# A hybrid attention and state-space block on one core: the attention branch's gate in blocks of 1024 columns, four of its sixteen k-tiles with seven tile products for eight

## Chip, core and metric

The kernel runs on one core of a Trainium2 chip. The metric is the device time of one execution in microseconds (us). Before the change the median of three runs is 1970.81 us (1970.03 to 1972.08).

Engines are named as in the profile: PE is TensorE (PEld its weight loads), DVE VectorE, ACT ScalarE, POOL GpSimd, SP SyncE.

## What is computed

One residual layer for a sequence of 256 tokens and a width of 2048, in float32: two token mixers side by side (sparse attention with a small indexer, and a Mamba-2 state-space mixer), each multiplied by a sigmoid gate, then a SwiGLU channel mixer and a last RMSNorm. The part that matters here:

```python
    gates = jax.nn.sigmoid(u @ w_gate).reshape(bsz, seq, 2, D_MODEL)
    merged = gates[:, :, 0] * (y_attn @ w_attn_branch) + gates[:, :, 1] * (y_ssm @ w_ssm_branch)
    return merged @ w_out
```

`u` is the normalized input (256 x 2048) and `w_gate` is 2048 x 4096. Its first 2048 columns are the gate of the attention branch.

## The kernel before

**A product in three matmuls.** Every float32 operand of the large gemms is split into a high part, rounded to the type that PE takes in one pass (an ACT copy), and a low part, the rest (a DVE subtraction). A tile product is then three matmuls that add into one psum buffer: high x high, high x low, low x high (L165 to L167). The 256 tokens are two token tiles t of 128; the contraction of 2048 is sixteen k-tiles of 128.

**A plain gemm** (`gemm`) computes 512 output columns: two psum buffers (one for each t), four loads of 1 MB on the SP queue (four k-tiles each, tile raw, three buffers), for each load two pairs of hi and lo tiles of 1024 columns (L196, L197), and 16 x 2 x 3 = 96 matmuls. The hi and lo tiles have four buffers each; behind the mixers every fifth pair lies in the pool xtra instead.

**Seven products.** The feed-forward gemms use `block7` with `fetch`: 1024 columns at once, as two blocks of 512. Four k-tiles are a quad. In a quad marked 1 two of its k-tiles, two token tiles and two column blocks form a 2 x 2 by 2 x 2 block product that Winograd's form of Strassen's scheme computes with seven tile products (numbered 1 to 7, each with a psum buffer) in place of eight. It needs sums of the left-hand tiles (slots 1, 8, 9, 12) and of the weights: `fetch` makes them on DVE as ta and tb (L749 to L751) and splits raw, tb and ta (L730, L731). The other two k-tiles of the quad, and quads marked 0, take eight products. When all is summed, DVE adds the psum buffers together into the four output blocks. The down projection (`down7`) has an eighth psum buffer, p8, for part of the eight-product terms.

**Order of work.** The instructions of each engine stand in a fixed order, which the framework's planner lays down when the program is built: it takes instructions as their operands and buffers come free by its own estimates, by priority, and priority is program order. Loads and splits of weights are raised by `high_priority`. PE, ACT, DVE and the SP and POOL queues each work through their order one by one.

**Around the change.** The attention loop runs over j = 0 to 3 (four heads each). For each j: a gemm for q (`w_m`), the transposes of q, and for t = 0, 1: logits lg (L618), masking into sc (L621), maximum (L626), exponentials (L629), division (L632, L633), transposes of sc (L641), their split into pT (L214, L215), and av (L645 to L647), which reads the value tile vh. av is split into ya_hi and ya_lo. Then comes a gemm of the state-space gate (`w_g`, blocks 4 to 7), evicted with a sigmoid at L655. Behind the loop the four blocks of the attention gate follow as plain gemms into the four tiles sga (a sigmoid at L667, `w_g` blocks 0 to 3), then the branch projection (`w_ab`, from ya_hi and ya_lo), the merge, the transposes of the merged tiles (`trans_split`), the output projection (`w_o`) with `quad_ops` for the left-hand operands of the feed-forward, and the feed-forward.

**Buffers.** The pool big has 11 tiles of 8 KB in a partition; u_hi, u_lo (two tiles each), acc (two), ya_hi, ya_lo (two each) and vh (one) are among them. The pool mid has 8 tiles of 4 KB. Psum: mm (4), trp (2, transposes and the like) and sdp (2, logits and av) up to the end of `w_o`; then they are closed and mmf (7) and trf (1) take their place, with waits tile by tile:

```python
    pctx.close()
    mm = ctx.enter_context(tc.tile_pool(name="mmf", bufs=7, space=bass.MemoryType.PSUM, reuse_waits="tile"))
    trp = ctx.enter_context(tc.tile_pool(name="trf", bufs=1, space=bass.MemoryType.PSUM, reuse_waits="tile"))
```

Of the kernel before, what the change touches and what calls it, by code (L numbers as in the profile page):

```python
# [8 lines left out]
F32 = mybir.dt.float32  # L9
# [5 lines left out]
P = 128  # L15
# [24 lines left out]
QUADS = (1, 1, 1, 0)  # L40

# [23 lines left out]
def hybrid_block(ctx, tc, xt, x, consts, cols, heads, gfin, w_a, w_i, w_m, w_g, w_ab, w_sb, w_o, w_f1, w_f2, out):  # L65
# [658 lines left out]
    def halves(raw, cuts):  # L724

        out = {}
        for i, n in cuts:
            hi, lo = (v[:, : n * 512] for v in hl_tiles())
            src = raw[:, i : i + n, :].rearrange("p k n -> p (k n)")
            nc.scalar.activation(hi, src, AF.Copy)  # L730
            nc.vector.tensor_tensor(lo, src, hi.bitcast(F32), ALU.subtract)  # L731
            for j in range(n):
                out[i + j] = hi[:, j * 512 : (j + 1) * 512], lo[:, j * 512 : (j + 1) * 512]
        return out

    nts = [0]

    def fetch(w, i, seven):

        with tc.high_priority(PRE):  # L740
            raw = wraw.tile([P, 4, 512], F32, tag="raw", name=nm("raw"))
            nc.sync.dma_start(raw.rearrange("p k n -> p (k n)"), w[i])
            if not seven:
                return halves(raw, ((0, 2), (2, 2)))
            b = halves(raw, ((0, 2),))
            nts[0] += 1
            ta = mid_t([P, 2, 512], name="ta")
            tb = mid_t([P, 2, 512], name="tb") if nts[0] % 2 else xtra[0].tile([P, 2, 512], F32, tag="tb", name=nm("tb"))
            nc.vector.tensor_tensor(ta, raw[:, 2:4, :], raw[:, 1:3, :], ALU.subtract)  # L749
            nc.vector.tensor_tensor(tb[:, 0, :], raw[:, 3, :], ta[:, 0, :], ALU.subtract)  # L750
            b["last"] = nc.vector.tensor_tensor(tb[:, 1, :], raw[:, 0, :], tb[:, 0, :], ALU.subtract)  # L751
            for base, t in ((6, tb), (4, ta)):
                for j, v in halves(t, ((0, 2),)).items():
                    b[base + j] = v
            b.update(halves(raw, ((3, 1),)))
            return b

# [29 lines left out]
    def block7(w, first, quads, get, ahead=None, after=None):  # L787

        n7 = sum(quads)
        n1 = 4 * len(quads) - 2 * n7
        left = {i: 3 * n7 for i in (1, 6, 7)}
        left.update({i: 3 * (n7 + n1) for i in (2, 3, 4, 5)})
        if after is not None:
            left[5], left[8] = 3 * n7, 3 * n1
        ps = {}

        def prod(i, a, b):
            start = i not in ps
            if start:
                ps[i] = tr_t([P, 512], "p8") if i == 8 else mm.tile([P, 512], F32, tag="mm", name=nm(f"p{i}"))
            with tc.issue_after(after) if i == 8 and start else nullcontext():
                for j, (x, y) in enumerate(((a[0], b[0]), (a[0], b[1]), (a[1], b[0]))):
                    left[i] -= 1
                    nc.tensor.matmul(ps[i], x, y, start=start and j == 0, stop=left[i] == 0)  # L808

        order = [(q, part) for q in range(len(quads)) for part in range(2)]  # L810
        if after is not None:
            order[1:3] = order[2:0:-1]
        for q, part in order:
            seven = quads[q] and part == 0
            if q == part == 0 and ahead is not None:
                b = ahead
            else:
                b = fetch(w, first + 2 * q + part, seven)
            if seven:
                prod(1, get(q, 0), b[1])  # L820
                prod(2, get(q, 2), b[0])
                prod(6, get(q, 9), b[6])
                prod(4, get(q, 3), b[7])
                prod(7, get(q, 1), b[5])
                prod(5, get(q, 8), b[4])
                prod(3, get(q, 12), b[3])
                continue
            k0 = 4 if quads[q] else 4 * part
            d0 = 10 if quads[q] else 8 + 2 * part
            a1, a2, d = (lambda k: k0 + 2 * k), (lambda k: k0 + 2 * k + 1), (lambda k: d0 + k)  # L830
            for i, slot, n in ((2, a1, 0), (4, a2, 0), *(((8, a2, 1), (3, a1, 1)) if after is not None else ((5, a2, 1), (3, d, 1)))):
                for k in range(2):
                    prod(i, get(q, slot(k)), b[2 * k + n])
        return ps
# [232 lines left out]
```

## Time and profile before

| | |
|---|---|
| median of three runs | 1970.81 us |
| the profiled execution | 1969.88 us, of which the span from the first to the last instruction is 1967.9 us |
| mean granted clock of PE | 0.998 |
| PE busy | 1954.5 us (99% of the span), 9095 matmuls |
| DVE, ACT busy | 1499.9 us (76%), 1066.8 us (54%) |
| read from HBM | 372 MB, 190 GB/s over the span |

How to read it: busy time of PE is from a matmul's start to its modelled end, and matmuls overlap, so one of 512 columns is listed with some 390 ns though they follow each other more closely. An engine's idle time is put down to what released it. `out<-in` are names of tiles, `mm<-hi,uh` a matmul into a buffer mm from the weights' tile hi and the left-hand tile uh.

### The profile page before, as it was taken

How to read it: one execution, taken by the hardware profiler on the slowest of the kernel's cores; microseconds unless marked ns; L12 is line 12 of the kernel's file. 1: busy time of each engine (PE TensorE's matmuls, PEld its weight loads, DVE VectorE, ACT ScalarE, POOL GpSimd, SP SyncE). 2: the span in 40 equal slices, each digit the busy share in tenths (PEclk: the TensorE clock that was granted, in tenths of full speed). 3: DMA queues.
4: the chain of work that ended last, by engine and by line, in shares of the span. 5: the costliest groups of instructions: out<-in, count | busy, mean ns of one | idle time of the engine just before them, and what ended most of it. 6: DMA issues, size and time to landing. Idle time of an engine off the chain costs nothing. (4 is left out here: it accounts for less than half of the span.)

```text
span 1967.9 us, 23619 instructions
## 1 busy us (share of the span) xinstructions
PE 1954.5 (99%) x9095; PEld 1619.2 (82%) x9095; DVE 1499.9 (76%) x2050; ACT 1066.8 (54%) x1291; POOL 36.2 (2%) x87
## 2 busy tenths in 40 slices
PE   9999999999999999999999999999999999999998
PEld 7898888888888888888888888788888888888886
DVE  7898867778778766666654556788989999899964
ACT  6575564654654544555554445565555665555553
POOL 0000000000000000000000000000000000000000
PEclk9999999999999999999999999999999999999999
DMA  7645555555554545544555555455545555555553
GB/s 276 233 151 177 189 195 187 190 195 171 193 203 160 193 171 192 182 163 168 185 185 195 184 193 206 154 198 212 193 178 208 213 194 213 192 195 213 212 193 128
DMA packets 54432, 375.71 MB, mean 191 GB/s; under 512 B 6304, under 2 KB 6816, under 8 KB 10672
## 3 DMA queue, kind: packets, MB, share of 16 engines
q1 hardware_dynamic: 51120, 360.86, 51.8%
q0 software_dynamic: 1968, 11.60, 1.7%
q10 hardware_dynamic: 1232, 1.75, 0.2%
q8 instruction: 71, 1.16, 0.2%
q14 instruction: 41, 0.34, 0.1%
HBM read 372.02 MB, written 2.16 MB: 190 GB/s over the span
## 5 line engine op out<-in xcount | busy, mean ns | idle before, releaser
L197 DVE TENSOR_TENSOR lo<-raw,hi 128x1024 fp32r<-128x1024 f32 (+3 forms) x449 | 540.5, 1207 | 314.6 <-ACT hi L196 313.1
L196 ACT ACTIVATE hi<-raw 128x1024 fp32r<-128x1024 f32 (+3 forms) x449 | 468.8, 1047 | 529.9 <-PE mm L167 463.4
L166 PE MATMUL mm<-lo,uh 128*128 128x512 f32 (+2 forms) x1184 | 461.0, 389 | 0.0
L167 PE MATMUL mm<-hi,ul 128*128 128x512 f32 (+2 forms) x1184 | 458.2, 388 | 0.2 <-DVE ul L218 0.2
L165 PE MATMUL mm<-hi,uh 128*128 128x512 f32 (+2 forms) x1184 | 453.2, 389 | 1.0 <-ACT hi L196 1.0
L730 ACT ACTIVATE hi<-raw 128x1024 fp32r<-128x1024 f32 x240 | 232.8, 978 | 138.7 <-PE p L808 103.0
L808 PE MATMUL p<-hi,opa 128*128 128x512 f32 x924 | 306.4, 390 | 0.0
L731 DVE TENSOR_TENSOR lo<-raw,hi 128x1024 fp32r<-128x1024 f32 x240 | 265.0, 1119 | 19.9 <-ACT hi L730 19.1
L165 PEld LDWEIGHTS mm<-hi,uh 128*128 128x128 f32 x1184 | 222.5, 188 | 44.5 <-ACT hi L196 1.9
L167 PEld LDWEIGHTS mm<-hi,ul 128*128 128x128 f32 x1184 | 222.8, 188 | 42.5 <-DVE ul L218 0.5
L166 PEld LDWEIGHTS mm<-lo,uh 128*128 128x128 f32 x1184 | 222.9, 188 | 41.0 <-DVE lo L197 0.3
L808 PEld LDWEIGHTS p<-hi,opa 128*128 128x128 f32 x924 | 173.4, 188 | 35.6
L808 PE MATMUL p<-lo,opa 128*128 128x512 f32 x462 | 180.9, 392 | 0.7 <-DVE lo L731 0.7
L808 PE MATMUL p<-hi,act 128*128 128x512 f32 x416 | 132.5, 390 | 0.0
L808 PE MATMUL p<-hi,opb 128*128 128x512 f32 x352 | 127.2, 391 | 1.0 <-ACT opf L695 0.8
L808 PEld LDWEIGHTS p<-lo,opa 128*128 128x128 f32 x462 | 86.7, 188 | 19.7 <-DVE lo L731 1.9
L166 PE MATMUL mm<-lo,yh 128*128 128x512 f32 x256 | 100.4, 392 | 0.0
L167 PE MATMUL mm<-hi,yl 128*128 128x512 f32 x256 | 100.4, 392 | 0.0
L165 PE MATMUL mm<-hi,yh 128*128 128x512 f32 x256 | 100.1, 395 | 0.0
L808 PEld LDWEIGHTS p<-hi,act 128*128 128x128 f32 x416 | 78.1, 188 | 16.4 <-ACT hi L730 0.3
L730 ACT ACTIVATE hi<-tb 128x1024 fp32r<-128x1024 f32 x45 | 47.7, 1059 | 76.7 <-PE p L808 45.7
L808 PE MATMUL p<-lo,act 128*128 128x512 f32 x208 | 80.6, 391 | 0.0
(283 smaller groups left out, 2533.2 us busy)
## 6 DMA issues: line engine op xcount, KB each, us to landing
raw<-in_w_f_dram SPq DMA_DIRECT2D x132, 1024.0 KB, 4.8
raw<-in_w_m_dram SPq DMA_DIRECT2D x104, 1024.0 KB, 4.8
raw<-in_w_sb_dram SPq DMA_DIRECT2D x32, 1024.0 KB, 4.8
raw<-in_w_g_dram SPq DMA_DIRECT2D x32, 1024.0 KB, 4.8
raw<-in_w_ab_dram SPq DMA_DIRECT2D x16, 1024.0 KB, 4.8
raw<-in_w_o_dram SPq DMA_DIRECT2D x16, 1024.0 KB, 4.8
abc<-acum_d POOLq DMA_DIRECT2D x8, 1024.0 KB, 5.2
raw<-in_w_i_dram SPq DMA_DIRECT2D x8, 768.0 KB, 4.3
```

Of the source, the lines that this page charges most:

```text
L165: nc.tensor.matmul(o, lh, rh, start=(kt == 0), stop=False)
L166: nc.tensor.matmul(o, lh, rl, start=False, stop=False)
L167: nc.tensor.matmul(o, ll, rh, start=False, stop=(kt == nk - 1))
L196: hi_ops.append(nc.scalar.activation(hi[:, o], src[:, o], AF.Copy))
L197: nc.vector.tensor_tensor(lo[:, o], src[:, o], hi[:, o].bitcast(F32), ALU.subtract)
L730: nc.scalar.activation(hi, src, AF.Copy)
L731: nc.vector.tensor_tensor(lo, src, hi.bitcast(F32), ALU.subtract)
L808: nc.tensor.matmul(ps[i], x, y, start=start and j == 0, stop=left[i] == 0)
```

## The change

The attention gate is computed as two blocks of 1024 columns by `block7`, with seven products for half of the first two quads (four of sixteen k-tiles) and the p8 buffer; the sums of the left-hand tiles, for four products of each of the two quads, are made ahead of it into a new tile uop of the pool big. The closing of the old psum pools and the opening of mmf and trf moves from the end of `w_o` to this place, and `halves`, `fetch` and `block7` move up with it, unchanged but for the argument eight (before, the argument after also stood for it). On the host the weights of these blocks are packed in the order that `fetch` reads. The core of it:

```diff
+GATE_QUADS = (1, 1, 0, 0)
...
     smx_ctx.close()
     xtra.append(ctx.enter_context(tc.tile_pool(name="xtra", bufs=1, reuse_waits="tile")))
-    sga = []
-    for nb in range(4):
-        ps = gemm(w_g, 4 * nb, 512, KT, lhs_u)
-        sg = mid_t([P, T, 512], name="sga")
-        for t in range(T):
-            nc.scalar.activation(sg[:, t, :], ps[t], AF.Sigmoid, scale=rs(t))
-        sga.append(sg)
+    pctx.close()
+    mm = ctx.enter_context(tc.tile_pool(name="mmf", bufs=7, space=bass.MemoryType.PSUM, reuse_waits="tile"))
+    trp = ctx.enter_context(tc.tile_pool(name="trf", bufs=1, space=bass.MemoryType.PSUM, reuse_waits="tile"))
...
+    uop = big_t([P, 2, 8, P], F32R, name="uop")
+    for q in range(sum(GATE_QUADS)):
+        f = mid_t([P, 8, P], name="uf")
+        i, j = divmod(4 * q, 8)
+        u_of = lambda a: a[i][:, j : j + 2, :].rearrange("p k (t n) -> p (k t) n", t=T)
+        nc.vector.tensor_tensor(f[:, 0:4, :], u_of(u_hi).bitcast(F32), u_of(u_lo).bitcast(F32), ALU.add)
+        nc.vector.tensor_tensor(f[:, 4, :], f[:, 1, :], f[:, 3, :], ALU.add)
+        nc.vector.tensor_tensor(f[:, 5, :], f[:, 4, :], f[:, 0, :], ALU.subtract)
+        nc.vector.tensor_tensor(f[:, 6, :], f[:, 0, :], f[:, 1, :], ALU.subtract)
+        nc.vector.tensor_tensor(f[:, 7, :], f[:, 2, :], f[:, 5, :], ALU.subtract)
+        split(uop[:, 0, 4 * q : 4 * q + 4, :], uop[:, 1, 4 * q : 4 * q + 4, :], f[:, 4:8, :])
+
+    def get_u(q, i):
+        if GATE_QUADS[q] and i in (1, 8, 9, 12):
+            j = 4 * q + {8: 0, 9: 1, 1: 2, 12: 3}[i]
+            return uop[:, 0, j, :], uop[:, 1, j, :]
+        return lhs_u(4 * q + i // 2, i % 2)
+
+    sga = [mid_t([P, T, 512], name="sga") for _ in range(4)]
+    for b in range(2):
+        ps = block7(w_g, 8 * b, GATE_QUADS, get_u, None, True)
+        x1, x4 = sga[2 * b][:, 0, :], sga[2 * b][:, 1, :]
+        x2, x3 = sga[2 * b + 1][:, 0, :], sga[2 * b + 1][:, 1, :]
+        with tc.high_priority(2 * PRE):
+            nc.scalar.activation(x1, ps[1], AF.Copy)
+            for o, i, v in ((x2, 6, x1), (x3, 7, x2), (x1, 2, x1), (x4, 4, x3), (x2, 5, x2), (x3, 5, x3), (x2, 3, x2), (x3, 8, x3)):
+                nc.vector.tensor_tensor(o, ps[i], v, ALU.add)
+        for x_, t in ((x1, 0), (x4, 1), (x2, 0), (x3, 1)):
+            nc.scalar.activation(x_, x_, AF.Sigmoid, scale=rs(t))
...
-    pctx.close()
-    mm = ctx.enter_context(tc.tile_pool(name="mmf", bufs=7, space=bass.MemoryType.PSUM, reuse_waits="tile"))
-    trp = ctx.enter_context(tc.tile_pool(name="trf", bufs=1, space=bass.MemoryType.PSUM, reuse_waits="tile"))
```

In `block7` a seven-product fetch issues the products in this order: 1 (slot 0), 2 (slot 2), 6 (slot 9), 4 (slot 3), 7 (slot 1), 5 (slot 8), 3 (slot 12). With the argument eight the fetches come as quad 0 seven, quad 1 seven, then the others.

## Rows read from the trace of the kernel before

**Rows 1.** The page: busy time of PE, and its granted clock by fortieths of the span.

```profile
PE 1954.5 (99%) x9095; PEld 1619.2 (82%) x9095; DVE 1499.9 (76%) x2050; ACT 1066.8 (54%) x1291; POOL 36.2 (2%) x87
...
PEclk9999999999999999999999999999999999999999
```

**Rows 2.** Waits of PE: who waited for whom, us in total, times, longest.

```profile
PE p L808 <- ACT opf L695: 0.8, 1, 0.8
PE p L808 <- DVE lo L731: 0.7, 2, 0.4
```

**Rows 3.** The chain of waits: start us, us, what (a piece from the feed-forward).

```profile
1441.77 124.15 PE p L808 x546
```

**Rows 4.** Busy time by stretch: PE, PEld, DVE, ACT, POOL, clock, DMA share, GB/s.

```profile
982.50:1018.50 36.00, 36.00 (x166) 29.93 (x165) 21.96 (x23) 21.43 (x30) 1.06 (x2) 1.00 0.56 190
1019.00:1095.00 76.00, 76.00 (x337) 62.95 (x336) 33.92 (x29) 33.60 (x35) 0.00 (x0) 1.00 0.56 194
```

**Rows 5.** The timeline of ACT about 982, and instructions on the tile vh.

```profile
982.18 0.69 ACT L655 ACTIVATE sg<-mm,rstd 128x512 f32<-128x512 f32 x1
...
L647 PE MATMUL av<-pT,vh x12: 389/393/397, 840.9 to 1018.1; 128*128 128x512 f32 x12
```

**Rows 6.** PE's timeline along the last attention group (start us, us, instruction).

```profile
984.99 0.60 PE L641 MATMUL tr<-kc,sc 128*128 128x128 f32 x4
991.13 0.39 PE L645 MATMUL av<-pT,vh 128*128 128x512 f32 x1
992.69 0.40 PE L647 MATMUL av<-pT,vh 128*128 128x512 f32 x1
998.39 1.02 PE L618 MATMUL lg<-kT,qT 128*128 128x256 f32 x4
1010.64 1.03 PE L641 MATMUL tr<-kc,sc 128*128 128x128 f32 x8
1016.07 0.39 PE L645 MATMUL av<-pT,vh 128*128 128x512 f32 x1
```

**Rows 7.** DVE by line from 1258 to 1282 (two seven-product fetches of the feed-forward).

```profile
L731 DVE TENSOR_TENSOR lo<-tb,hi 128x1024 fp32r<-128x1024 f32 x2 | 2.4, 1224 | 0.1
L749 DVE TENSOR_TENSOR ta<-raw 128x1024 f32<-128x1024 f32 x2 | 2.4, 1222 | 0.6 <-DMA raw<-in_w_f_dram 0.6
L750 DVE TENSOR_TENSOR tb<-raw,ta 128x512 f32<-128x512 f32 x2 | 1.4, 685 | 0.0
```

**Rows 8.** DVE's timeline along the last attention group.

```profile
987.49 0.68 DVE L215 TENSOR_TENSOR pT<-tr,pT 128x512 fp32r<-128x512 f32 x1
993.94 0.68 DVE L215 TENSOR_TENSOR yal<-av,yah 128x512 fp32r<-128x512 f32 x1
1001.09 1.22 DVE L626 TENSOR_REDUCE mx<-sc 128x4 f32<-128x1024 f32 x1
1006.47 1.23 DVE L633 TENSOR_TENSOR sc<-sc,den 128x1024 f32<-128x1024 f32 x1
1012.22 1.28 DVE L215 TENSOR_TENSOR pT<-tr,pT 128x512 fp32r<-128x512 f32 x2
```

**Rows 9.** ACT's timeline along it, and its instructions on the tile yah.

```profile
1002.85 1.28 ACT L629 ACT_TABLE_LOAD   x1
1004.14 0.51 ACT L629 ACTIVATE sc<-sc,mx 128x256 f32<-128x256 f32 x1
1006.04 0.19 ACT L629 ACTIVATION_READ_ACCUMULATOR sc<-sc,mx 128x1 f32 x1
...
L214 ACT ACTIVATE yah<-av x8: 597/597/601, 841.3 to 1018.5; 128x512 fp32r<-128x512 f32 x8
```

**Rows 10.** Busy time by stretch behind PE's last matmul, columns as in rows 4.

```profile
1961.00:1968.00 7.00, 0.00 (x0) 0.00 (x0) 1.76 (x6) 0.72 (x1) 0.33 (x1) 0.56 0.41 150
```

**Rows 11.** PE's timeline at the kernel's start, about the rise of the clock.

```profile
8.41 0.87 PE L165 MATMUL mm<-hi,uh 128*128 128x400 f32 x2
...
9.95 0.53 PE L165 MATMUL mm<-hi,uh 128*128 128x400 f32 x2
```

More of the change, by code (lines that the diff above doesn't have):

```diff
@@ new lines, in halves, with fetch @@
+    def halves(raw, cuts):
+        out = {}
+        for i, n in cuts:
+            hi, lo = (v[:, : n * 512] for v in hl_tiles())
+            src = raw[:, i : i + n, :].rearrange("p k n -> p (k n)")
+            nc.scalar.activation(hi, src, AF.Copy)
+            nc.vector.tensor_tensor(lo, src, hi.bitcast(F32), ALU.subtract)
+            for j in range(n):
+                out[i + j] = hi[:, j * 512 : (j + 1) * 512], lo[:, j * 512 : (j + 1) * 512]
+        return out
+    nts = [0]
+    def fetch(w, i, seven):
+        with tc.high_priority(PRE):
+            raw = wraw.tile([P, 4, 512], F32, tag="raw", name=nm("raw"))
+            nc.sync.dma_start(raw.rearrange("p k n -> p (k n)"), w[i])
+            if not seven:
+                return halves(raw, ((0, 2), (2, 2)))
+            b = halves(raw, ((0, 2),))
+            nts[0] += 1
+            ta = mid_t([P, 2, 512], name="ta")
+            tb = mid_t([P, 2, 512], name="tb") if nts[0] % 2 else xtra[0].tile([P, 2, 512], F32, tag="tb", name=nm("tb"))
+            nc.vector.tensor_tensor(ta, raw[:, 2:4, :], raw[:, 1:3, :], ALU.subtract)
+            nc.vector.tensor_tensor(tb[:, 0, :], raw[:, 3, :], ta[:, 0, :], ALU.subtract)
+            b["last"] = nc.vector.tensor_tensor(tb[:, 1, :], raw[:, 0, :], tb[:, 0, :], ALU.subtract)
+            for base, t in ((6, tb), (4, ta)):
+                for j, v in halves(t, ((0, 2),)).items():
+                    b[base + j] = v
+            b.update(halves(raw, ((3, 1),)))
+            return b
@@ new lines, in block7, with prod @@
+    def block7(w, first, quads, get, ahead=None, eight=False, after=None):
+        n7 = sum(quads)
+        n1 = 4 * len(quads) - 2 * n7
+        left = {i: 3 * n7 for i in (1, 6, 7)}
+        left.update({i: 3 * (n7 + n1) for i in (2, 3, 4, 5)})
+        if eight:
+            left[5], left[8] = 3 * n7, 3 * n1
+        ps = {}
+        def prod(i, a, b):
+            start = i not in ps
+            if start:
+                ps[i] = tr_t([P, 512], "p8") if i == 8 else mm.tile([P, 512], F32, tag="mm", name=nm(f"p{i}"))
+            with tc.issue_after(after) if i == 8 and start and after is not None else nullcontext():
+                for j, (x, y) in enumerate(((a[0], b[0]), (a[0], b[1]), (a[1], b[0]))):
+                    left[i] -= 1
+                    nc.tensor.matmul(ps[i], x, y, start=start and j == 0, stop=left[i] == 0)
+        order = [(q, part) for q in range(len(quads)) for part in range(2)]
+        if eight:
+            order[1:3] = order[2:0:-1]
+        for q, part in order:
+            seven = quads[q] and part == 0
+            if q == part == 0 and ahead is not None:
+                b = ahead
+            else:
+                b = fetch(w, first + 2 * q + part, seven)
+            if seven:
+                prod(1, get(q, 0), b[1])
+                prod(2, get(q, 2), b[0])
+                prod(6, get(q, 9), b[6])
+                prod(4, get(q, 3), b[7])
+                prod(7, get(q, 1), b[5])
+                prod(5, get(q, 8), b[4])
+                prod(3, get(q, 12), b[3])
+                continue
+            k0 = 4 if quads[q] else 4 * part
+            d0 = 10 if quads[q] else 8 + 2 * part
+            a1, a2, d = (lambda k: k0 + 2 * k), (lambda k: k0 + 2 * k + 1), (lambda k: d0 + k)
+            for i, slot, n in ((2, a1, 0), (4, a2, 0), *(((8, a2, 1), (3, a1, 1)) if eight else ((5, a2, 1), (3, d, 1)))):
+                for k in range(2):
+                    prod(i, get(q, slot(k)), b[2 * k + n])
+        return ps
@@ L722, in quad_ops @@
         return get
[L724 to L756, printed above, removed]
     lhs_m = lhs_quads(mT)
@@ L780, in hybrid_block @@
     nc.vector.tensor_copy(rstd2, rstd_of(ssq2, D, "rs0"))
-    pctx.close()
-    mm = ctx.enter_context(tc.tile_pool(name="mmf", bufs=7, space=bass.MemoryType.PSUM, reuse_waits="tile"))
-    trp = ctx.enter_context(tc.tile_pool(name="trf", bufs=1, space=bass.MemoryType.PSUM, reuse_waits="tile"))
     sq5 = sm.tile([P, T, 5], F32, tag="sq5", bufs=1, name="sq5")
[L787 to L834, printed above, removed]
     def act_ops(src, seven, ext):
@@ L894, in down7 @@
         for b in range(2):
-            ps = block7(w_f2, first + 2 * len(quads) * b, quads, lambda q, i: gets[q](i), None, after)
+            ps = block7(w_f2, first + 2 * len(quads) * b, quads, lambda q, i: gets[q](i), None, True, after)
             xa, xb = ev_t([P, T, 512], "xa"), ev_t([P, T, 512], "xb")
```

10 lines of the change are left out of this document (6 added, 4 removed).

## The prediction

> **What bounds the kernel now.** I read the page first. TensorE (PE) is busy 99% of the span at a granted clock of 0.9 or more of full speed in every slice [rows 1]. The view of PE's waits has only seven lines, the two largest behind the kernel's start 0.8 and 0.7 us [rows 2]. So the kernel is a stream of matmuls: an edit is worth what it takes out of that stream, less every gap that it opens in it. PE has nothing in reserve to catch up with, so an opened gap goes straight into the time. The price of one matmul of 512 columns comes from the chain of waits, where 546 in a row take 124.15 us, 0.2274 us each [rows 3].
>
> Then I read what lies around the edited loop, in the order of time. VectorE (DVE) is busy 33.9 of 76 us while the four gate blocks run [rows 4], so there is room for the added subtractions. The last attention group (j = 3) is not over when these blocks begin. The loop's last gate gemm is evicted from 982.18 us on, so PE is done with it at about 982.5. The last read of the value tile vh is at 1018.1 [rows 5]. In those 36 us PE is busy throughout, with 166 matmuls [rows 4]. The attention's own are 29 of them (8 for logits, 12 transposes, 9 for av); the other 137 belong to the four gate blocks and are strewn between. They are what hides the softmax chain. That is the place to watch.
>
> **Removed matmuls.** A block of 1024 columns has two quads with 15 products and two with 16, 62 products of three matmuls, 186; two blocks make 372 where four blocks of 512 made 384. Saved: 12 x 0.2274 = 2.7 us, all on PE's path.
>
> **DVE and ScalarE (ACT) work added.** A seven-product fetch adds one ta (1.22 us), two halves of tb (0.69 each), the low parts of tb and ta (1.22 each) and splits three rather than four k-rows directly (0.69 + 1.22 instead of 2.45): 4.5 us, four times, 18 us [rows 7]. The left-hand sums are some five DVE operations per quad, 5 us in all. The eviction has 8 adds per block at 0.68, 11 us. 33.9 + 18 + 5 + 11 = 68 us of about 76: still below PE. I cost it at nothing; the cover is PE's remaining 80 us of matmuls. If two seven-product fetches in a row (about 13 us of DVE against 9.5 us of PE) outran the buffers, it would cost up to 3.5 us per block. Against that stands the feed-forward stage, where the same fetches run with a DVE wait of 0.7 us in all [rows 2]. The SP queue issues the same sixteen loads of 1 MB; none is moved.
>
> **Psum pools.** All later gemms get seven buffers instead of four, and transposes get one instead of two. With one buffer the second four transposes wait for the first four's eviction; the feed-forward already does this (L846), and no line of PE's waits names a wait there [rows 2]. I take 0, at worst 1 us over eight places. The old pools were closed ahead of the feed-forward. There the third product waited 0.82 us for the eviction of a transpose buffer (opf, L695) whose place it takes [rows 2]. That wait goes: -0.8 us (between 0 and -1.3, if the 0.4 us that is late next, a DVE low part, goes with it).
>
> **The gap.** Three things now keep gate matmuls from filling the attention's tail.
> First, uop is a tile of the pool big (11 buffers). Live at that point are u_hi and u_lo (4), acc (2), ya_hi and ya_lo (4) and vh (1): eleven. So uop must take vh's place and can't be written before the last av matmul, the one at 1018.1 [rows 5]. Products 6, 7, 5 and 3 of a seven-product fetch read uop; only 1, 2 and 4 don't.
> Second, the fetch's blocked products keep their hi and lo tiles (four buffers and one in xtra). The first fetch keeps three, so the second gets through 1, 2 and 4 at most, and the third can't be split. That leaves 18 matmuls, 4.1 us, where 137 stood.
> Third, the products' psum buffers lie where lg, av and tr lie, and each must wait for the attention to leave it.
> So PE runs dry after 982.5 until the attention ends and uop is split.
>
> How long is that? I follow the chain through the rows, leaving out the stretches in which an operation was ready and PE merely came to it late (988.17 to 991.13, 994.62 to 998.39, 1007.70 to 1010.64, 1013.50 to 1016.07, together 12.2 us), since an idle PE isn't late [rows 6, 8, 9]:
> transposes to pT's low part, 984.99 to 988.17: 3.18; three av matmuls 0.85; yah and yal, 993.09 to 994.62: 1.53; the second logits 1.02; masking and maximum, 999.41 to 1002.31: 2.90; exponentials and division, to 1007.70: 5.39; eight transposes and both pT, 1010.64 to 1013.50: 2.86; six av matmuls 1.53. Sum 19.3. Then yah, uop's high and low part: 0.60 + 0.60 + 0.69 = 1.9. Together 21.2 us.
> PE's own attention work in it is 0.60 + 0.85 + 2 x 1.02 + 1.03 + 1.53 = 6.05. If the 18 matmuls run ahead of the chain, PE idles 21.2 - 6.05 = 15.1 us; if they lie in its gaps, 11.0.
> The lower end: this chain shares DVE and ACT with weight splits, one of each per 2.7 us. Without them and the table load ahead of the exponentials [rows 9], four terms fall: 3.18 to 0.60 + 0.60 + 0.68 = 1.88, 1.53 to 0.60 + 0.68 = 1.28, 2.90 to 0.69 + 1.22 = 1.91, and 5.39 to 2.09 (1004.14 to 1006.23) + 0.2 + 1.23 = 3.5. In all 16.8 us, idle 16.8 - 6.05 - 4.1 = 6.6.
> With no free filler, a full buffer set stops the splits, which speeds the chain, while two seven-product fetches' worth of DVE work comes first, which slows it. I take 12 us, near the pace of the rows. Behind the blocked product 6 stands everything on PE; nobody else waits.
>
> **Sum**, against the profiled execution's 1969.88 us (span 1967.9): 1969.9 - 2.7 - 0.8 + 12 = 1978.4. The median of the runs shown is 0.9 above that execution, so 1979.3.
>
> **A rule weighed against a row.** The granted clock is at full through the whole body. After PE's last matmul, in the stretch 1961 to 1968, its mean is 0.56, so it has dropped to the lower level of 1.2 GHz for most of it [rows 10]. The longest gap here, from the second logits to the eight transposes, is 8.3 us of idle PE. No row shows an idle PE inside the body.
> The Trainium skill (TensorE: Matmul & The Clock Gate, section "Why this matters for your kernels") asks that PE not be left idle between bursts of matmuls, or the clock falls back to half. By it the rival "clock" below comes true, 1982.8 instead of 1979.3; the trace's end agrees in direction.
>
> **Rivals.**
> *The gap is hidden (0.15).* The planner finds uop a place earlier, or the attention's tail is issued earlier, so that its end meets the end of the loop's last gemm. For it: operations stood ready for 12 us before PE came. Against it: eleven live tiles in eleven buffers. Then 1969.9 - 3.5 = 1966.4, 1967.3 as a median. The place is product 6's wait for uop; break-even is a gap of 3.5 us. This is the not-slower side.
> *Short gap (0.17).* The chain runs undisturbed and all 18 matmuls lie in it: 6.6 - 3.5 = +3.1, 1973.9.
> *Clock (0.15).* The eight transposes, the six av matmuls and the first products run at half rate. At the start of the kernel two matmuls of 400 columns, 0.87 us from the first's start to the second's end with 0.54 for one, come 0.33 us apart at the lower level; later, with 0.53 and 0.35, they come 0.18 apart [rows 11], so each costs almost double: 1.0 + 1.5 for the transposes and av, 1 to 2 for the products: +3.5 on the forecast, 1982.8.
> *Long gap (0.08).* The order on ACT and DVE puts other work ahead and the chain keeps its present pace, late stretches included: 21.2 + 12.2 - 6.05 = 27, 1969.9 - 3.5 + 27, 1994.3.
> *Forecast (0.45).* A gap of 9 to 15 us.
>
> **How the numbers follow.** About 0.2% (3.9 us) is what a measurement here can tell from no change. Hidden and short gap both end within it, except that a hidden gap with 1.3 instead of 0.8 us gained at the feed-forward comes near -0.2%: faster 0.04, same 0.28. The other three are slower: 0.68. The range runs from the hidden gap to the forecast's long end with the clock (15 - 3.5 + 3.5 on 1970.8), 1967 to 1986; outside lie the long gap and a little at either end. The likeliest case's own range is 1976 to 1983.
>
> **What would show it.** Right: PE waits at L808 on DVE (uop's low part), on psum eviction or at the attention's lines, summing to 9 to 15 us between about 980 and 1010; the last av matmul some 15 us earlier than 1018; 9083 matmuls in place of 9095; no wait of 0.8 us at the first feed-forward products. Wrong: gate products 6 and 7 running before the last av matmul, or PE's waits there under 3.5 us. The clock rival shows as matmuls 0.43 us apart behind the longest gap. A sum that misses by DVE waits inside the gate blocks would say that the added splits weren't covered.

## The result and the profile after

The changed kernel takes 1989.08 us (median of five runs, 1987.09 to 1989.76) against 1971.35 us (1970.03 to 1972.62) for the kernel before on the same chip: ratio 1.0088, 95% interval 1.0076 to 1.0099. It is slower, as forecast, but by 17.7 us and not by 8.5, and above the range's end of 1986. The profiled execution took 1989.08 us with a span of 1987.1 us, so it stands at the median.

First the page of the changed kernel: busy times, and PE's granted clock by fortieths of the span (compare [rows 1]).

```profile
PE 1960.2 (99%) x9083; PEld 1621.6 (82%) x9083; DVE 1529.6 (77%) x2098; ACT 1074.4 (54%) x1303; POOL 37.5 (2%) x87
...
PEclk9999999999999999999989999999999999999999
```

Twelve matmuls are gone, worth 2.7 us, yet PE's busy time rose by 5.7 us: the remaining matmuls were busy 8.4 us longer in all. One slice of the clock, the one about 1000 us, is no longer at 9.

The waits of PE in the changed kernel (who waited for whom: us, times, longest), in place of [rows 2]:

```profile
PE tr L642 <- DVE sc L634: 5.7, 1, 5.7
PE p L722 <- DVE lo L674: 5.2, 2, 3.9
PE p L722 <- ACT hi L673: 2.0, 2, 1.6
PE mm L166 <- ACT hi L197: 1.3, 1, 1.3
PE av L647 <- DVE pT L216: 1.3, 1, 1.3
...
PE av L646 <- ACT pT L215: 0.8, 1, 0.8
```

The wait for opf is gone, as forecast. The waits of the transposes, of av and of the products for high parts (hi) are new, and the products' wait for low parts (lo) was 0.7 us before. PE's timeline in the attention's tail (start us, us, instruction, idle time before it and what ended it) says where, beside [rows 6]:

```profile
983.67 0.50 PE L646 MATMUL av<-pT,vh 128*128 128x512 f32 x1 [0.83 <-ACT pT L215]
...
985.82 1.13 PE L619 MATMUL lg<-kT,qT 128*128 128x256 f32 x4 [0.32 <-DVE sc L622]
992.66 1.94 PE L642 MATMUL tr<-kc,sc 128*128 128x128 f32 x8 [5.71 <-DVE sc L634]
...
998.10 0.50 PE L647 MATMUL av<-pT,vh 128*128 128x512 f32 x1 [1.29 <-DVE pT L216]
998.43 0.40 PE L648 MATMUL av<-pT,vh 128*128 128x512 f32 x1
998.67 0.39 PE L722 MATMUL p<-hi,uh 128*128 128x512 f32 x1
...
1004.51 0.80 PE L722 MATMUL p<-lo,uh 128*128 128x512 f32 x1 [3.90 <-DVE lo L674]
1005.11 0.63 PE L722 MATMUL p<-hi,ul 128*128 128x512 f32 x1
1005.53 0.63 PE L722 MATMUL p<-hi,uh 128*128 128x512 f32 x1
```

The five gaps sum to 12.05 us, the forecast's 12. Three things differ from it. No product of the gate stands ahead of the last av matmul (18 were expected there); the first follows directly behind it, at 998.67. The last gap, 3.90 us, lies behind the attention and is for a low part of the second fetch's weights on DVE; no gap is a wait for uop. And matmuls of 512 columns follow each other at 0.43 us at 1005, not at 0.227. The windows of the changed kernel show that as the granted clock (stretch; its length, PE, PEld, DVE, ACT, POOL busy; clock; DMA share; GB/s):

```profile
985.00:990.00 5.00, 1.63 (x7) 0.74 (x5) 3.29 (x4) 2.91 (x7) 0.21 (x1) 1.00 0.38 105
990.00:995.00 5.00, 2.34 (x9) 1.86 (x9) 1.99 (x3) 1.94 (x7) 0.00 (x0) 0.50 0.00 0
995.00:1000.00 5.00, 3.71 (x12) 2.25 (x11) 5.00 (x11) 2.76 (x5) 0.00 (x0) 0.82 0.00 0
1000.00:1005.00 5.00, 1.10 (x3) 0.67 (x3) 5.00 (x9) 1.60 (x3) 0.00 (x0) 0.86 0.09 20
1005.00:1010.00 5.00, 5.00 (x13) 3.79 (x13) 5.00 (x9) 3.21 (x5) 0.00 (x0) 0.50 0.46 190
1287.00:1293.00 6.00, 4.67 (x11) 3.29 (x12) 6.00 (x9) 1.75 (x2) 0.00 (x0) 0.50 0.06 11
```

The clock is at its lower level (0.50, 1.2 GHz) in 990 to 995 and in 1005 to 1010, and once more at the start of the feed-forward. The Trainium skill (TensorE: Matmul & The Clock Gate, section "Wait — 56ns, not 53.3ns?") gives 426.7 ns from start to start for 512 columns at the lower level; the rows above agree with 0.42 us (1005.11 to 1005.53).

The windows also show DVE busy for all of 995 to 1010. Its timeline says with what:

```profile
974.46 1.23 DVE L674 TENSOR_TENSOR lo<-raw,hi 128x1024 fp32r<-128x1024 f32 x1 [2.92 <-ACT hi L673]
...
994.41 0.69 DVE L216 TENSOR_TENSOR pT<-tr,pT 128x512 fp32r<-128x512 f32 x1 [1.90 <-ACT pT L215]
995.02 1.28 DVE L756 TENSOR_TENSOR uf<-uh,ul 128x512 f32<-128x512 f32 x2
996.22 1.22 DVE L692 TENSOR_TENSOR ta<-raw 128x1024 f32<-128x1024 f32 x1
...
1003.24 1.22 DVE L674 TENSOR_TENSOR lo<-raw,hi 128x1024 fp32r<-128x1024 f32 x1
...
1005.58 0.48 DVE L760 TENSOR_TENSOR uf<-uf 128x128 f32<-128x128 f32 x2
```

The first products' operands were there at 975.7 (974.46 + 1.23), 23 us ahead of their first use. The left-hand sums uf and the first ta begin only at 995, between the writing of the last two pT (DVE's low part of the second is at 997.36). uop follows them: ACT's split of it starts at 1005.9, right behind the last uf and some 7 us after the last av matmul had left vh. The first matmul that reads it follows at 1006.81 without a wait.

At the feed-forward's start PE's timeline has three gaps, 3.34 us together, and the low clock behind them:

```profile
1285.33 0.50 PE L722 MATMUL p<-hi,opa 128*128 128x512 f32 x1 [1.56 <-ACT hi L673]
...
1286.80 0.72 PE L722 MATMUL p<-hi,opa 128*128 128x512 f32 x1 [0.45 <-ACT hi L673]
1288.85 0.79 PE L722 MATMUL p<-lo,opa 128*128 128x512 f32 x1 [1.33 <-DVE lo L674]
1289.44 0.63 PE L722 MATMUL p<-hi,opa 128*128 128x512 f32 x1
```

The kernel before has 1.58 us there (0.10, 0.24 and these two), at a clock of 1.00:

```profile
1259.12 0.50 PE L808 MATMUL p<-hi,opb 128*128 128x512 f32 x1 [0.82 <-ACT opf L695]
...
1274.35 0.50 PE L808 MATMUL p<-lo,opa 128*128 128x512 f32 x1 [0.42 <-DVE lo L731]
```

ACT's timeline just ahead of the changed kernel's gaps shows the last transposes late:

```profile
1275.78 0.84 ACT L806 ACTIVATE opf<-tr,colp 128x256 f32<-128x256 f32 x2
1281.49 0.84 ACT L806 ACTIVATE opf<-tr,colp 128x256 f32<-128x256 f32 x2 [4.87 <-PE tr L803]
```

The last quad's first transposes were evicted by 1276.6; the second set stands on PE only at 1280.85, 4.2 us later, with products ahead of it. So the order on PE holds it back, not a wait for the one transpose buffer during the run; whether the planner chose that order because of the one buffer is what two of the experiments ask. Its sums, and the seven-product fetches behind them on DVE, then come late.

**The account of the span**, 1967.9 to 1987.1, +19.2: matmuls -2.7; waits in the tail +12.05; waits at the feed-forward's start +1.76; other waits -0.4; busy time of the remaining matmuls +8.4. Of the last, the lower clock explains about 7, by an estimate from the rows: 1.8 for the transposes and av behind the 5.71 us gap (from the run with filled gaps below), 2.9 for the fourteen matmuls from 1004.51 to 1010.56 (6.05 us in place of 14 x 0.2274), some 2.3 at the feed-forward's start (eleven or twelve at 0.43 instead of 0.23). The rest, about 1.4, fits the ends of the gaps, where a matmul is listed with its whole 0.39 to 0.50 us because no other overlaps it; it wasn't measured by itself.

### The profile page after: what moved, and what is told of

It reads as the page before. It is cut to its first block, busy times and chain, and to the rows that moved or that the text cites. A ratio compares the mean times of both kernels' runs of the same rounds, so it can differ in the third digit from the quotient of the medians.

```text
span 1987.1 us, 23663 instructions
## 1 busy us (share of the span) xinstructions
PE 1960.2 (99%) x9083; PEld 1621.6 (82%) x9083; DVE 1529.6 (77%) x2098; ACT 1074.4 (54%) x1303; POOL 37.5 (2%) x87
## 4 chain that ended last, share of the span: by engine, by line
PE 98%; DVE 1%; issue 1%; ACT 0%; DMA 0%; POOLq 0%; POOL 0%; DVEq 0%; ACTq 0%
PE p L722 36%; PE mm L166 19%; PE mm L167 19%; PE mm L168 19%; PE yp L517 1%; PE lg L619 1%; PE tr L431 1%; PE tr L871 0%; PE tr L540 0%; PE tr L494 0%; PE tr L642 0%; PE tr L585 0%; DVE lo L674 0%; PE tr L803 0%; DMA colp<-in_cols_dram 0%
## 5 line engine op out<-in xcount | busy, mean ns | idle before, releaser
L198 DVE TENSOR_TENSOR lo<-raw,hi 128x1024 fp32r<-128x1024 f32 (+3 forms) x417 | 501.2, 1205 | 268.4 <-ACT hi L197 266.7
L197 ACT ACTIVATE hi<-raw 128x1024 fp32r<-128x1024 f32 (+3 forms) x417 | 434.8, 1045 | 481.0 <-PE mm L168 413.0
L167 PE MATMUL mm<-lo,uh 128*128 128x512 f32 (+2 forms) x1056 | 411.1, 389 | 0.0
L168 PE MATMUL mm<-hi,ul 128*128 128x512 f32 (+2 forms) x1056 | 408.2, 387 | 0.0
L166 PE MATMUL mm<-hi,uh 128*128 128x512 f32 (+2 forms) x1056 | 403.2, 389 | 1.3 <-ACT hi L197 1.3
L673 ACT ACTIVATE hi<-raw 128x1024 fp32r<-128x1024 f32 (+1 forms) x272 | 263.5, 981 | 171.8 <-PE p L722 133.8
L674 DVE TENSOR_TENSOR lo<-raw,hi 128x1024 fp32r<-128x1024 f32 (+1 forms) x272 | 300.9, 1122 | 38.6 <-ACT hi L673 37.9
L166 PEld LDWEIGHTS mm<-hi,uh 128*128 128x128 f32 x1056 | 198.5, 188 | 39.6 <-ACT hi L197 2.2
L168 PEld LDWEIGHTS mm<-hi,ul 128*128 128x128 f32 x1056 | 198.9, 188 | 37.0 <-issue 0.2
L692 DVE TENSOR_TENSOR ta<-raw 128x1024 f32<-128x1024 f32 x49 | 59.8, 1221 | 28.9 <-DMA raw<-in_w_f_dram 26.0
```

The source lines that it names most:

```text
L166: nc.tensor.matmul(o, lh, rh, start=(kt == 0), stop=False)
L167: nc.tensor.matmul(o, lh, rl, start=False, stop=False)
L168: nc.tensor.matmul(o, ll, rh, start=False, stop=(kt == nk - 1))
L197: hi_ops.append(nc.scalar.activation(hi[:, o], src[:, o], AF.Copy))
L198: nc.vector.tensor_tensor(lo[:, o], src[:, o], hi[:, o].bitcast(F32), ALU.subtract)
```

## Experiments

Two theories for the empty tail. **A, the pool move:** with the old psum pools closed ahead of the gate, the planner puts everything in the new ones behind the old pools' last tiles. **B, the change's own tiles:** uop, uf and the blocked fetches can't be made before the attention has left its tiles, as forecast. Beside them stood the clock and the single transpose buffer. "Excess" below is the median less that of the kernel before, run on the same chip with it.

| kernel | us (lowest to highest) | ratio, 95% interval | excess |
|---|---|---|---|
| pools moved, gate plain | 1990.54 (1989.34 to 1990.87) | 1.0099, 1.0083 to 1.0114 | +20.1 |
| first half plain in the old pools | 1981.67 (1980.23 to 1982.40) | 1.0053, 1.0036 to 1.0070 | +11.2 |
| change, two transpose buffers again | 1985.92 (1984.92 to 1987.88) | 1.0077, 1.0062 to 1.0092 | +15.4 |
| change, gaps filled | 1987.99 (1987.41 to 1988.58) | 1.0087, 1.0072 to 1.0102 | +17.5 |
| change in the old pools | 1985.62 (1984.24 to 1986.23) | 1.0072, 1.0060 to 1.0085 | +14.6 |
| the same, uf in ev | 1983.89 (1982.81 to 1985.07) | 1.0065, 1.0052 to 1.0077 | +12.9 |
| half plain, half seven, old pools | 1973.97 (1971.79 to 1975.58) | 1.0014, 1.0005 to 1.0023 | +3.0 |
| half plain, three sets of pools | 1976.10 (1973.51 to 1978.31) | 1.0024, 1.0015 to 1.0033 | +5.1 |
| pools moved behind the plain gate | 1978.60 (1977.50 to 1981.45) | 1.0042, 1.0029 to 1.0056 | +7.4 |
| old pools, plain quads first | 1980.03 (1978.36 to 1980.77) | 1.0044, 1.0031 to 1.0057 | +8.8 |
| the same, uf in ev | 1972.70 (1971.66 to 1974.93) | 1.0007, 0.9999 to 1.0016 | +1.5 |
| the same, fetches spread | 1975.50 (1974.83 to 1979.11) | 1.0024, 1.0013 to 1.0034 | +4.3 |

### The pool move alone

```diff
-    for b in range(2):
-        ps = block7(w_g, 8 * b, GATE_QUADS, get_u, None, True)
...
+    for nb in range(4):
+        ps = gemm(w_g, 4 * nb, 512, KT, lhs_u)
```

The pools are closed where the change closes them; the gate stays four plain gemms with all 384 matmuls.

> The psum pools are closed at the new place, but the gate stays four plain gemms of 512 columns (384 matmuls, no sums, no uop). Theory A, the new pools are what keeps gate matmuls out of the attention's tail: PE again runs no gate matmul before the last av, waits about 8 us there (0.8 + 0.3 + 5.7 + 1.3 as in the changed kernel), loses 1.6 us to the low clock behind it, and the start of the feed-forward costs about 5 us more than before (1.8 of waits, 3.2 of half-rate matmuls): 1971 + 8 + 1.6 + 5 = 1986. Theory B, uop's wait for vh and the sums of the seven-product fetches make the gap: gate matmuls fill the tail as before, only the start of the feed-forward is worse, 1976.

Measured: +20.1 us, more than the whole change and 4.5 us above theory A's 1986. PE's timeline of this kernel in the tail:

```profile
985.07 0.50 PE L646 MATMUL av<-pT,vh 128*128 128x512 f32 x1 [2.06 <-ACT pT L215]
...
994.14 1.94 PE L642 MATMUL tr<-kc,sc 128*128 128x128 f32 x8 [5.79 <-DVE sc L634]
...
998.51 0.43 PE L648 MATMUL av<-pT,vh 128*128 128x512 f32 x1
998.78 0.39 PE L166 MATMUL mm<-hi,uh 128*128 128x512 f32 x1
```

Plain gemms, which need nothing but u and a psum buffer, don't run ahead of the last av either. A alone empties the tail. The tail's waits are 7.85 us, as theory A had them. At the feed-forward's start this kernel waits 0.26 + 2.68 + 3.41 us, more than was expected, again with a lower clock.

### The first half plain, ahead of the pool move

```diff
+    for nb in range(2):
+        ps = gemm(w_g, 4 * nb, 512, KT, lhs_u)
...
     pctx.close()
...
-    for b in range(2):
+    for b in range(1, 2):
```

> The first 1024 gate columns are two plain gemms in the old psum pools, which are closed behind them; the second 1024 columns take seven products (six matmuls fewer than before). Theory A: the plain gemms fill the attention's tail, no wait there, 1.4 us saved, the feed-forward's start costs 5 us as in the changed kernel: 1975. Theory B (the seven-product fetches' work on DVE leaves PE short by itself): a wait of about 4 us on DVE's low parts where the seven-product block begins, and the low clock behind it: 1979 to 1982.

Measured: +11.2 us. The tail is full (PE busy for all of 980 to 1030). What is left are a wait of 2.38 us where the block with seven products starts (1036.55, for ACT's high part) and one of 7.38 us at the feed-forward's start (1278.71, with the single transpose buffer), where the clock falls too. The time lies in theory B's interval, but not for its reason: the wait at the block is shorter than the 4 us expected and the clock stays at 1.00 behind it.

### Two transpose buffers again for the projections

```diff
     lhs_ya = lhs_of(ya_hi, ya_lo)
...
+    pctx.close()
+    mm = pctx.enter_context(tc.tile_pool(name="mmo", bufs=4, ...))
+    trp = pctx.enter_context(tc.tile_pool(name="tro", bufs=2, ...))
```

The change as it is, with seven and one buffers opened once more ahead of the feed-forward.

> The changed kernel with the seven and one psum buffers closed behind the gate; four mm and two transpose buffers stand again for the branch and output projections, and the pools of the feed-forward open where they did before. Theory A (with one transpose buffer the last quad's second transposes come late, the fetch behind them too, and PE starves at the feed-forward's start): that part of 5 us goes, 1984. Rival (the late fetch there has another cause, the attention's gap or the moved schedule): no change, 1989.

Measured: 1985.92 us, between the two expectations; the intervals of this and of the change overlap, so the traces decide. Span 1984.0 against 1987.1. At the feed-forward's start the gaps are 0.11, 0.24, 0.84, 0.20 and 0.17, as before, and the clock is at 1.00 from 1275 to 1295. The gaps in the tail are the change's to within 0.01 us. So that part of the loss, 2 to 3 us (excess 15.4 against 17.7; spans 3.1 apart), goes with the buffers (four and two for seven and one; the transpose buffer alone wasn't varied) and is separate from the tail.

### The gaps filled with matmuls of zeros

```diff
+            if j == NKV - 1 and t == 1:
+                wa = sd_t([P, 512], name="wa")
+                for i in range(24):
+                    nc.tensor.matmul(wa, wz[:, :P], wz, start=True, stop=True)
```

And 14 more behind the last av; they add work whose result nobody reads.

> The changed kernel with 24 matmuls on a tile of zeros put behind the last logits and 14 behind the last av; nothing reads what they write. If the gaps cost more than their own length because PE's clock falls to the lower level in them: the granted clock stays at full through the tail, the eight transposes and the av matmuls behind the gap run at 0.113 and 0.227 us apart, the gate's first matmuls at 0.227 instead of 0.427, and the time falls by 1.6 + 2.8 us to 1984.7. If the half-rate stretch has another cause, or the added matmuls stand in the way of the real ones: 1989 or more.

Measured: 1987.99 us, not told apart from the change and in neither expectation (1984.7, or 1989 and more). The windows:

```profile
990.00:995.00 5.00, 3.91 (x20) 1.93 (x18) 3.79 (x6) 2.23 (x8) 0.00 (x0) 1.00 0.00 0
995.00:1000.00 5.00, 4.39 (x20) 2.43 (x21) 5.00 (x11) 3.01 (x4) 0.00 (x0) 1.00 0.02 3
1000.00:1005.00 5.00, 2.54 (x8) 1.77 (x7) 5.00 (x10) 2.05 (x3) 0.00 (x0) 0.78 0.26 69
```

The clock stays at 1.00 up to 1000, and the last av matmul starts at 996.64 in place of 998.43. But then PE waits 2.46 us for DVE (1003.23), which is busy without a break from 995, and the clock is down again in 1000 to 1005 (0.78). The lower clock in the first gap was real, about 1.8 us of it on av's path. Giving it back shortens the span by 1.1 us only (1986.0 against 1987.1), not by the 4.4 expected: DVE's queue then sets the pace, and the added matmuls themselves hold the gate's first product back to 999.72 (998.67 in the change).

### The change without the pool move

```diff
-    pctx.close()
-    mm = ctx.enter_context(tc.tile_pool(name="mmf", bufs=7, ...))
...
+    psd[0] = lambda i: (mm.tile(...) if i in (1, 2, 6, 4)
+        else sd_t([P, 512], f"p{i}") if i in (7, 5) else tr_t([P, 512], f"p{i}"))
```

The products' eight buffers come from the old pools, which close ahead of the feed-forward.

> The change as it is (two blocks with seven products, uop and its sums, 12 matmuls saved), but the old psum pools stay open until the feed-forward: the products' eight buffers come from mm (1, 2, 6, 4), sdp (7, 5) and trp (3, 8). If moving the pools is the only cause, the tail is filled as before and the time is 1970.5 - 2.7 = 1968 us, at most 1970. If the change's own tiles (uop and its sums behind the last pT and vh) close the tail as well, as forecast, only products 1 and 2 of the first fetch (6 matmuls, 1.4 us) run ahead, the waits of 12.05 us fall to 10 or 11, half-rate stretches of 3 to 5 us stay, the feed-forward's start is as before: 1983 to 1986 us, about that of the kernel with two transpose buffers again.

Measured: +14.6 us, a time within the second expectation: without the pool move the tail is empty too, as theory B says. PE's timeline:

```profile
984.11 0.40 PE L720 MATMUL p<-hi,ul 128*128 128x512 f32 x1
...
994.61 1.94 PE L642 MATMUL tr<-kc,sc 128*128 128x128 f32 x8 [5.71 <-DVE sc L634]
...
1006.47 0.79 PE L720 MATMUL p<-lo,uh 128*128 128x512 f32 x1 [3.18 <-DVE lo L672]
```

Only products 1 and 2 of the first fetch, six matmuls ending with the first row, run ahead of the tail; then nothing that can run is left. The tail's waits sum to 12.4 us; they didn't fall to 10 or 11, as was expected. The feed-forward's start is as before (0.10, 0.24, 0.84, 0.46). A and B each empty the tail, and their costs don't add.

### The sums out of the pool mid

```diff
-        f = mid_t([P, 8, P], name="uf")
+        f = ev_t([P, 8, P], "uf")
```

> As the run before, with uf (the sums' float32 tile) in the pool ev instead of mid, so that the sums needn't stand behind the last pT. If uop waits only for its sums, uop is split before the last transposes, the other products run ahead of the last av and the tail's waits fall below 5 us: 1974 to 1978 us. If uop's place is vh's, as forecast, uop's split still stands behind the last yah and yal; the last wait shrinks by 1 to 4 us because DVE has done the sums early: 1980 to 1984 us.

Measured: 1983.89 us, in the second expectation's interval; the ranges of this and of the run before overlap. With uf in mid the changed kernel's first sums were made at 995.0; here the first sums are made at 981.0 and the last at 988.2. uop's split doesn't follow them. The instructions on the tile uop (count; ns; first and last start):

```profile
L215 ACT ACTIVATE uop<-uf x2: 618/619/620, 1001.7 to 1002.2; 128x512 fp32r<-128x512 f32 x2
```

It comes 1.1 us after the modelled end of the last av matmul (1000.6), 13 us after the sums were ready. That is what the forecast's first reason, vh's place, asks for. It isn't shown by this alone: on ACT the split stands directly behind the last yah (1001.25), and a kernel with uop in another place wasn't tried. In the change itself the sums were later than vh and hid this.

### Half plain, half with seven products

First in the old pools all the way (the two edits above together, one block of 1024 with seven products, 6 matmuls fewer than before):

> First 1024 columns as two plain gemms (192 matmuls), the second 1024 with seven products in the old pools, which stay open until the feed-forward: 6 matmuls fewer than before. If the cause is only what stands in the attention's tail, the tail is filled by the plain gemms, waits stay below 1.5 us in all and the clock at full: 1970.5 - 1.4 = 1969, at most 1971. If the pool ev or DVE is what bounds at the block's start, a wait of 2 to 3 us stands there: 1971 to 1972.

Then with the pools of the change for the block alone, four and two for the projections, seven and one for the feed-forward:

> First 1024 columns plain in the old pools, then the pools closed and seven and one buffers opened for the second 1024 with seven products, then four and two again for the branch and output projections, seven and one again for the feed-forward. Both parts of the loss (tail, feed-forward start) should go: 1969 to 1972 us, with a wait of about 2.4 us at the block's start left from the run with the half alone. If closing pools costs by itself wherever it stands, each of the three places shows waits of 1 us or more and the time stays above 1974.

Measured: +3.0 us, above both intervals, and +5.1 us, a time of the second expectation (above 1974) without the waits that it asks for at each pool change. In the first, PE's waits there are one line:

```profile
PE p L727 <- ACT hi L678: 2.8, 1, 2.8
```

It lies at 1035.43, where the seven-product fetch begins; the tail is full, the clock at 1.00. The trace's span is 1970.2: +2.8 for this wait, -1.4 for the matmuls; the other 0.9 of its excess of 2.3 is not in PE's waits and stays open. With three sets of pools the same wait is 2.38 and no pool change shows a wait of its own over 0.8 us. One difference is in the trace: behind that wait the clock is at 0.50 from 1036 to 1038, where the first of the two kernels has 1.00, and PE is busy 1.9 us longer in all (1955.9 against 1954.0). Why the median stands 4 us above the upper end of 1972 isn't settled by that.

### The pools moved behind a plain gate

```diff
-    for b in range(2):
-        ps = block7(...)
+    for nb in range(4):
+        ps = gemm(w_g, 4 * nb, 512, KT, lhs_u)
...
+    pctx.close()
     lhs_ya = lhs_of(ya_hi, ya_lo)
```

> The gate as four plain gemms (384 matmuls, as before), with the psum pools closed directly behind it instead of behind the output projection: the rest of the pool move, without its part in the attention's tail. If the single transpose buffer is what costs at the feed-forward's start, the tail is filled, the waits there stay below 1 us, and the feed-forward's first products wait 2 to 4 us in all with the clock partly at the lower level: 1973 to 1977 us. If the loss there came from the gate's blocks being late (everything pushed against the feed-forward), it goes with them: 1970 to 1972 us.

Measured: +7.4 us, a little over the first expectation; the waits at the feed-forward's start are 6.35 us, not the 2 to 4 expected. The tail is full (10.00 of 10 us in each window from 980 to 1070). PE's timeline at the feed-forward's start:

```profile
1272.00 0.80 PE L719 MATMUL p<-lo,opa 128*128 128x512 f32 x1 [2.68 <-DVE lo L671]
...
1276.63 0.80 PE L719 MATMUL p<-hi,opb 128*128 128x512 f32 x1 [3.41 <-ACT hi L670]
```

So the pool move has two prices at two places: the tail, and the projections' end with seven and one buffers.

### Something to run in the tail

```diff
-GATE_QUADS = (1, 1, 0, 0)
+GATE_QUADS = (0, 0, 1, 1)
...
+            [(0, 0), (0, 1), (1, 0), (1, 1), (2, 0), (3, 0), (2, 1), (3, 1)],
```

The change's arithmetic in the old pools, with seven products for quads 2 and 3; the first block's plain quads come first (the added line is its order of quad and half), and the products are dealt out to the old pools in another way (mm 2, 4, 8, 3; sdp 1, 6; trp 7, 5).

> The change's arithmetic (372 matmuls in the gate), in the old psum pools (closed ahead of the feed-forward), with seven products for quads 2 and 3 instead of 0 and 1 and with the eight-product quads first in the first block: 96 matmuls that need only u and four buffers stand at the attention's tail. If the cause is only that nothing that can run stands there, the tail's waits fall from 12 to below 4 us (a wait for uop's sums behind the last pT may stay), the clock stays at full, 1968 to 1972 us. If the seven-product fetches outrun DVE whatever the order, waits of 4 to 8 us come at the first seven-product fetch instead: 1974 to 1980 us.

> As the run before, with uf in the pool ev, so that the sums are made ahead of the last pT. If the last pT holds the sums up, uop's wait shrinks by up to 3 us against the run before: 1967 to 1970 us, at or just below the kernel before. If DVE's work is bound in total there, no difference: within 1 us of the run before.

Measured: +8.8 us with uf in mid, at the upper end of the second expectation; +1.5 with uf in ev, above the first expectation and far below the second. In the first kernel the tail is full up to the transposes, and one wait of 4.40 us follows the last av (1016.54), for the high part of tb. DVE is busy for all of 1010 to 1020, and the sums of uf (first at 1007.6, last at 1016.1) stand there among the last pT, ta and tb. In the second, with the sums made from 982 to 988, PE's timeline is

```profile
1007.73 1.03 PE L642 MATMUL tr<-kc,sc 128*128 128x128 f32 x8
...
1012.56 0.50 PE L720 MATMUL p<-hi,uop 128*128 128x512 f32 x1 [1.21 <-ACT uop L215]
...
1014.02 0.80 PE L720 MATMUL p<-hi,uop 128*128 128x512 f32 x1 [0.73 <-ACT hi L671]
```

Eight transposes take 1.03 us, not 1.94. The gap of 5.71 us and that of 3.9 are gone, and the wait for uop is 1.21 us. That one edit of a pool was worth 7.3 us, against at most 3 expected. With 12 matmuls fewer this kernel can't be told from the one before: 2.2 us of these waits and a stretch at half clock behind them (0.50 in 1014 to 1016) make up some 4 us, more than the 2.7 saved.

### The fetches spread

```diff
-            [(0, 0), (0, 1), (1, 0), (1, 1), (2, 0), (3, 0), (2, 1), (3, 1)],
+            [(0, 0), (0, 1), (1, 0), (1, 1), (2, 1), (2, 0), (3, 1), (3, 0)],
```

In the second block, seven-product and plain fetches take turns.

> As the run with plain quads first and uf in the pool ev, with the fetches in another order: first block quads 0 and 1 plain, then second half of quad 2 (eight products, 24 matmuls that need only u), its seven products, second half of quad 3, its seven products; second block with seven-product and plain fetches in turn. If the rest of the loss is the 2.2 us of waits for uop and for ACT's high parts and the half-rate stretch behind them, both go, no wait over 0.5 us stays in the gate and the time is what the matmuls alone give, 1971.0 - 2.7 = 1968.3 us (1968 to 1970). If the block change then waits for the psum eviction (p1, p2 of the second block), 1 to 3 us come back: 1970 to 1973 us.

Measured: +4.3 us, above both intervals. The wait for uop is gone, but PE's waits begin with

```profile
PE p L720 <- DVE sga L783: 3.6, 2, 1.8
PE p L720 <- DVE lo L672: 1.3, 3, 1.0
```

The seven-product fetch now ends the first block, so the second block's products wait for the adds that empty their psum buffers (1033.68 and 1039.58), and the clock is at 0.81 in 1030 to 1040. No version here beats the kernel before.

## Why the prediction missed

**What failed.** Three terms were put at nothing or below it. The lower clock had no place in the sum and took about 7 us. The pools' term was -0.8 us; the waits at the feed-forward's start grew by 1.76 us instead, and 2.3 of the 7 us lie there. The added DVE work was put at nothing, and 3.90 us of the tail's gap are a wait for it; the sum for the gap met 12 all the same.

**Right.** 12 matmuls saved, 2.7 us. The sign, and the place: the fill of the attention's tail. The gap's size: 12.05 us measured, 12 taken. The last av matmul at 998.4, 20 us earlier than before (15 were named).

**The gap's working was partly wrong where its sum was right.** That 12.05 us met the 12 is in part luck. Up to the last av the waits are 8.15 us, and the longest is 5.71, not 8.3; the other 3.90 is the DVE wait, a term that was put at nothing, and product 6 didn't wait for uop. The 18 matmuls of filler were none. The third reason named the psum buffers' places; the pool move does empty the tail by itself (+20.1), but the plain gemm's first operands and buffers alone don't explain why nothing at all was issued ahead; what in the planner sets that order stays open. The first reason, uop in vh's place, agrees with the two kernels with uf in ev without being shown by them; in the change it was covered by the sums, which the prediction costed at nothing.

**"I cost it at nothing" failed at one place.** The cover named for DVE's work was PE's remaining 80 us of matmuls, 68 of 76 us busy. Behind the tail the work comes at once: sums, two ta, tb, low parts, with DVE busy for all of 995 to 1010, and PE's 3.9 us wait there is for it. A busy share over 76 us hid a queue 15 us long. By the prediction's own terms two seven-product fetches are 13.9 us of DVE (2 x 6.95), not 13, and outrun PE's 9.5 by 4.4 us, not 3.5.

**The psum-pools term had the wrong sign.** -0.8 us was taken: nothing for the single transpose buffer, because it caused no wait in the feed-forward, less the wait for opf [rows 2]. The wait for opf did go. But ahead of the feed-forward the transposes of the merged and projected tiles sit on the path to its first operands, and there waits rose by 1.76 us and the half clock added some 2.3: +4.1 in the change's trace, 2 to 3 us when the buffers alone are put back, and +7.4 when this part of the move is made alone. The rows used were from another stage than the one that changed.

**The clock was a rival and should have been a term.** The forecast itself had 8.3 us of PE idle in it, and [rows 10] showed the clock fall in an idle PE. Put into the sum with its own estimate, 3.5, it gives 1982.8. The rows give about 7 us, 4.7 in the tail and 2.3 at the feed-forward's start, which wasn't expected to have gaps. The rule that the prediction weighed is the Trainium skill's (TensorE: Matmul & The Clock Gate, section "Why this matters for your kernels"): an idle PE between bursts of matmuls brings the clock back to half. The trace agrees at the three places, where the clock is at 0.50.

By these steps: 1969.9 - 2.7 + 12.05 + 1.8 - 0.4 + 8.4 = 1989.05, against 1989.08 for the profiled execution. The sum closes by construction, since 8.4 is what PE's busy time leaves over. The miss of 9.8 us is the longer matmuls (8.4, about 7 of it the clock) and the pools' term (2.6), less the other waits (0.4) and the 0.9 by which the forecast stood above its own sum; the gap's size is not in it. This is an account and not a promise: with the tail's gaps filled, little of the clock's part came back.

## What to carry to other kernels

Before a loop is replaced that fills another stage's waits, ask what of the new loop can be issued during those waits: the operands, each tile's pool and the order in which buffers are handed out. Here closing the psum pools early cost more than the twelve matmuls could give (+20.1 us alone), and so did a sums tile in the wrong pool in one order of the fetches (7.3 us; 1.7 in the change's order). Where PE has no other work, price a gap at its length and allow for the matmuls behind it at half clock, and check DVE's load over the few microseconds where the work falls due, not over the stage.

## What the runs showed of the hardware

For the shorter waits, whether the lower clock followed could not be told from their length. In the kernel with plain quads first and uf in ev, waits of 0.25, 1.21 and 0.73 us (at 1009.0, 1012.6 and 1014.0) came with a clock of 0.50 in 1014 to 1016, with 512 columns at 0.43 us. In the half-plain kernel in the old pools a single wait of 2.77 us was followed by 1.00. In the half-plain kernel with three sets of pools the same place has a wait of 2.38 us, ending at 1035.29, and 0.50 behind it. The run with the first half plain has a wait of 2.38 us there too, ending at 1036.55, and the clock stays at 1.00 from 1036 to 1040. The rows, from the windows of the four kernels, in this order:

```profile
1014.00:1016.00 2.00, 1.98 (x5) 1.57 (x6) 2.00 (x3) 2.00 (x3) 0.96 (x2) 0.50 0.80 315
```

```profile
1036.00:1038.00 2.00, 2.00 (x10) 1.65 (x10) 2.00 (x3) 1.36 (x2) 0.00 (x0) 1.00 0.41 78
```

```profile
1036.00:1038.00 2.00, 2.00 (x7) 1.53 (x6) 2.00 (x3) 1.23 (x2) 0.00 (x0) 0.50 0.48 106
```

```profile
1036.00:1040.00 4.00, 3.45 (x15) 2.72 (x16) 4.00 (x6) 2.50 (x4) 0.00 (x0) 1.00 0.45 139
```

So the length of such a wait did not tell, in these runs, whether the clock fell behind it: two waits of 2.38 us at the same place ended differently.
